# Gate phase of a hybrid decoder block: two additions made by accumulating transfers in place of VectorE

## Chip, cores and metric

One of the eight cores of a Trainium2 chip runs the program. The metric is the device time of one execution in microseconds, the median of several runs.

The core's engines run on their own and wait for each other by semaphores. In the profile PE is TensorE (PEld its weight loads), DVE is VectorE, ACT is ScalarE, POOL is GpSimd and SP is SyncE, which here only issues transfers. Each engine takes its instructions in the order in which they are written.

## Reference

The kernel computes one decoder block over 2048 tokens of width 1024. Attention and a linear recurrence run side by side; their joined output is projected, normalised and added to the input; last, a gate adds a normalised embedding. Only the end matters here:

```python
mix = jnp.concatenate([y_attn, y_lru], axis=-1) @ w_out[i]
h = h + rmsnorm(mix, post_gain[i])
e = rmsnorm(p[i] @ w_ple[i], ple_gain[i])
gate = jax.nn.sigmoid(h @ w_ple_gate[i] + b_ple_gate[i])
h = h + gate * e
```

All of it is float32, and the result is (1, 2048, 1024).

## The kernel before

The kernel works through its stages one after the other: the projections, the attention, the recurrence, the output projection, and last the gate phase, which the change is about. Every float32 operand of a matmul is split into a high and a low part, and each product is made of three matmuls (lines 66 to 68).

**The calendar.** From the output projection on, the program is written in slots. `plan(slot, phase, f)` puts a piece of work into a slot; within a slot the phases come in the order LOAD, COMBINE, PREP, JOB, MUL, GATE, STORE, and `run_slots` writes the pieces out in that order. A slot holds 12 matmuls of TensorE. This order is the order in which each engine and SP's queue take their work; the pieces themselves start when their semaphores allow.

**The gate phase** goes through 16 blocks of 128 tokens (TB = 16, n is the block). Block n's matmuls take slots s to s + 3, with s = G0 + 4n. For each block `plan_gate(n)` plans:

- `load_m` (slot s - 8; s - 10 and s - 7 for blocks 0 and 1): SP loads the projected row block from `m_d` into `mt` (2 buffers) and the input row block from `x` into `xt` (4 buffers), 512 KB each;
- `squares` (s - 6): ACT squares and sums `mt`, DVE and POOL make the factor `rs` of the norm (lines 150 and 151);
- `residual` (s - 5): DVE scales `mt` by the factor and the gain (L1777) and adds it to `xt`; `xt` is now h;
- `turn` and `turn_split` (s - 3 and s - 2): PE transposes `xt` (L1785), ACT copies the high part `h` out of the bank (L52), DVE makes the low part (L58);
- `load_e` (s - 2): SP loads the embedding's row block into `et`, one of two buffers;
- `mul` (s to s + 3): PE's 96 matmuls, two halves of 512 columns each in its bank `pbank`;
- `bias` (two slots after a half's start): DVE adds the bias to the bank, ACT takes the sigmoid (L1813);
- `finish_`: DVE multiplies gate, embedding and its norm's factor (L1817), then adds `xt`; the sum is the result, and SP stores it from `et` (L1843) in the same slot.

Additions by the helper `tt` all carry line 1629. `X`, `XT`, `MT` and `MR` are lists of buffers, and some of their names are shared: `XT[1]` is `X[11]`, so the profile shows that row as `X`. The last block is cut into halves of 512, 256 and 256 columns.

Of the kernel before, what the change touches and what calls it, by code (L numbers as in the profile page):

```python
# [11 lines left out]
AF = mybir.ActivationFunctionType  # L12
ALU = mybir.AluOpType
# [8 lines left out]
TB = S // P  # L22
# [14 lines left out]
LOAD, COMBINE, PREP, JOB, MUL, GATE, STORE = range(7)  # L37
# [12 lines left out]
def split(nc, src, hi, lo, eh, el):  # L50
    if eh == "act":
        nc.scalar.activation(hi, src, AF.Copy)  # L52
    elif eh == "dve":
        nc.vector.tensor_copy(hi, src)
    else:
        nc.gpsimd.tensor_copy(hi, src)
    eng = nc.vector if el == "dve" else nc.gpsimd
    eng.tensor_tensor(out=lo, in0=src, in1=f32(hi), op=ALU.subtract)  # L58


def mm3(nc, out, ws, xs, start, stop):


    wh, wl = ws
    xh, xl = xs
    nc.tensor.matmul(out, lhsT=wh, rhs=xh, start=start, stop=False)  # L66
    nc.tensor.matmul(out, lhsT=wh, rhs=xl, start=False, stop=False)  # L67
    nc.tensor.matmul(out, lhsT=wl, rhs=xh, start=False, stop=stop)  # L68
# [3 lines left out]
def hymba_kernel(ctx: ExitStack, tc: tile.TileContext, x, xT, pT, w_p, w_v, w_o, w_ple, w_pg,  # L72
                 w_gates, vecs, rows, mgrp, out):
    nc = tc.nc
# [10 lines left out]
    m_d = dram.tile([S, D], F32, name="m_d")  # L85
# [61 lines left out]
    def rsqrt_small(o, ss, pool, n):  # L147

        t = pool.tile([P, n], F32, name=f"rs{n}", bufs=2)
        nc.vector.tensor_scalar(t, ss, 1.0 / D, EPS, ALU.mult, ALU.add)  # L150
        nc.gpsimd.tensor_tensor(out=o, in0=t, in1=mhalf[:, :n], op=ALU.pow)  # L151
# [51 lines left out]
    def plan(slot, phase, f):  # L203


        assert (slot, phase) >= tuple(now), (slot, phase, now)
        order_[0] += 1
        heapq.heappush(calendar.setdefault(slot, []), (phase, order_[0], f))
# [415 lines left out]
    sg, vp, lw, s = [None], [None], [None, None], {}  # L624
# [731 lines left out]
    for h in range(1, NH):  # L1356
        base = t0[4 * (h - 1)]
        for p_ in range(8):
            a = base + (13, 16, 26, 28, 31, 33, 36, 38)[p_]
# [12 lines left out]
    for i, (n, k) in enumerate([(0, k) for k in range(KD)] + [(1, k) for k in range(5)]):  # L1372
        a = last0 + 2 * i
# [119 lines left out]
    X, banks = [], {}  # L1493

    def bank3():
        return ps3.tile([P, 512], F32, name="bank3")
# [62 lines left out]
    G_ = Ctx()  # L1559
# [34 lines left out]
    MR, U2_, U3_, XT, MT, A1 = [], [], [], [], [], []  # L1594
# [21 lines left out]
    def product_bank():  # L1616
        return G_.pse.tile([P, 512], F32, name="pbank")
# [11 lines left out]
    tt = lambda o, x, y, op: nc.vector.tensor_tensor(out=o, in0=x, in1=y, op=op)  # L1629
# [94 lines left out]
    for n in range(1, 12):  # L1724
        for k in range(KD):
            if n == 1 and k < 5:
                continue
            s = k - 4 if n == 1 else 11 + 3 * k // 2 if n == 2 else w_starts[n - 1] + k
# [30 lines left out]
    def plan_gate(n):  # L1759
        s = G0 + 4 * n  # L1760
        ts = slice(n * P, (n + 1) * P)
        u = Ctx()
        c_load = s - (10, 7)[n] if n < 2 else s - 8

        def load_m():
            u.mt, u.xt = MT[n % 2], XT[n % 4]
            nc.sync.dma_start(out=u.mt, in_=m_d[ts, :])
            nc.sync.dma_start(out=u.xt, in_=x[ts, :])

        def squares():  # L1770
            u.ss = G_.small.tile([P, 1], F32, name="ss", bufs=2)
            u.rs = G_.small.tile([P, 1], F32, name="rsm", bufs=2)
            nc.scalar.activation(X[8], u.mt, AF.Square, accum_out=u.ss)
            rsqrt_small(u.rs, u.ss, G_.small, 1)

        def residual():
            nc.vector.scalar_tensor_tensor(out=u.mt, in0=u.mt, scalar=u.rs, in1=G_.pgain,  # L1777
                                           op0=ALU.mult, op1=ALU.mult)
            tt(u.xt, u.mt, u.xt, ALU.add)

        def turn(q):
            b = u.b = bank3()
            for k in range(4):
                kk = 4 * q + k
                nc.tensor.transpose(b[:, k * P:(k + 1) * P], u.xt[:, kk * P:(kk + 1) * P], ident)  # L1785

        def turn_split(q):
            if q == 0:
                if n < 2:
                    G_.h[n] = [G_.r3.tile([P, 512], F32R, name=f"h{n}{i}", tag=f"mr{i}" if n else f"U{i}", bufs=1)  # L1790
                               for i in range(4)]
                h = G_.h[n % 2]
                u.h = [(h[0], h[1]), (h[2], h[3])]
            split(nc, u.b, u.h[q][0], u.h[q][1], "act", "dve")

        def mul(a, z, ks):
            if ks[0] == 0:
                u.bank = product_bank()
            for k in ks:
                c = slice(k % 4 * P, (k % 4 + 1) * P)  # L1800
                hh, hl = u.h[k // 4]
                mm3(nc, u.bank[:, :z - a], (hh[:, c], hl[:, c]), (wG[k][0][:, a:z], wG[k][1][:, a:z]),
                    k == 0, k == KD - 1)

        def load_e():
            u.et = X[9 + n % 2]
            nc.sync.dma_start(out=u.et, in_=e_d[ts, :])

        def bias(a, z, b):
            u.gt = MR[4 + turn_[0] % 4][:, :z - a]  # L1810
            turn_[0] += 1
            tt(u.gt, b[:, :z - a], G_.bgate[:, a:z], ALU.add)
            nc.scalar.activation(u.gt, u.gt, AF.Sigmoid)  # L1813
            return u.gt

        def finish_(a, z, gt):
            nc.vector.scalar_tensor_tensor(out=u.et[:, a:z], in0=gt, scalar=rstd_e[:, n:n + 1],  # L1817
                                           in1=u.et[:, a:z], op0=ALU.mult, op1=ALU.mult)
            tt(u.et[:, a:z], u.et[:, a:z], u.xt[:, a:z], ALU.add)

        plan(c_load, LOAD, load_m)
        plan(s - 6, JOB, squares)
        plan(s - 5, JOB, residual)
        for q in range(2):
            plan(s - 3 + q, GATE, lambda q=q: turn(q))
            plan(s - 3 + q, GATE, lambda q=q: turn_split(q))
        plan(s - 2, LOAD, load_e)
        cuts = ((0, 512), (512, 1024)) if n < TB - 1 else ((0, 512), (512, 768), (768, 1024))
        for j, (a, z) in enumerate(cuts):
            b_ = []  # L1830
            if z - a == 512:
                for m in range(2):
                    plan(s + 2 * j + m, MUL, lambda a=a, z=z, m=m: mul(a, z, range(4 * m, 4 * m + 4)))
                e = s + 2 * j + 2
            else:
                plan(s + 1 + j, MUL, lambda a=a, z=z: mul(a, z, range(KD)))
                e = s + 2 + j
            plan(e - 1, STORE, lambda b_=b_: b_.append(u.bank))
            g_ = []
            plan(e, COMBINE, lambda a=a, z=z, b_=b_, g_=g_: g_.append(bias(a, z, b_[0])))  # L1840
            plan(e, JOB, lambda a=a, z=z, g_=g_: finish_(a, z, g_[0]))
            plan(e, STORE if n < TB - 1 else JOB,
                 lambda a=a, z=z: nc.sync.dma_start(out=out[ts, a:z], in_=u.et[:, a:z]))  # L1843

    G_.small, G_.h = w1, {}
    for n in range(TB):
        plan_gate(n)
# [67 lines left out]
```

## Time and profile before

| | us |
|---|---|
| median of 3 runs | 2120.77 |
| lowest and highest | 2119.97, 2121.5 |
| the profiled execution | 2120.41 |
| its span, first to last instruction | 2118.6 |

TensorE's mean granted clock was 0.995 of full speed. The gate phase's transposes and matmuls stand in the span from about 1918 us to its end.

The page slices the span into 40 equal parts; each digit is the busy share of a slice in tenths:

```profile
PE   8799999999999999999999999999999999999999
DVE  7777997696758877896578888888885678776665
POOL 4834554332203334733026656566542000000000
DMA  8498898988788889887757776777744777665553
```

TensorE is nearly full throughout. POOL, which works in the first three quarters, does hardly anything in the last nine slices. In the gate phase SP's queue is the only one that kernel transfers run on.

### The profile page before, as it was taken

Reading aid. Unit: us, or ns where it says so; the run is one execution under the profiler, and the core shown is the slowest. Engines: PE = TensorE matmul, PEld = TensorE weight load, DVE = VectorE, ACT = ScalarE, POOL = GpSimd, SP = SyncE. Lnnn points to the kernel's source line nnn. Section 1 sums busy time; section 2 is a strip of 40 time slices with the busy share of each in tenths; the row PEclk is TensorE's granted clock in tenths of the full one; section 3 lists DMA queues with packets and bytes.
Section 4 is the critical chain, followed back from the end, with each engine's and each line's share of the span. In section 5 each row is a group of like instructions: output and inputs, shape, how many; then the busy total and the mean of one; then the engine's idle time right before and its main releaser. Section 6 shows DMA issues by size and latency. Waiting matters only on the chain.

```text
span 2118.6 us, 31621 instructions
## 1 busy us (share of the span) xinstructions
PE 2084.5 (98%) x10586; PEld 1744.3 (82%) x10586; DVE 1619.9 (76%) x2693; ACT 1144.9 (54%) x1871; POOL 736.2 (35%) x633
## 2 busy tenths in 40 slices
PE   8799999999999999999999999999999999999999
PEld 6788888888988888888878888888887888888887
DVE  7777997696758877896578888888885678776665
ACT  7435765443327776565267776777774344442232
POOL 4834554332203334733026656566542000000000
PEclk9999999999999999999999999999999999999999
DMA  8498898988788889887757776777744777665553
GB/s 319 180 313 294 291 347 304 343 322 308 268 276 270 279 254 299 268 280 259 267 180 225 230 210 222 235 228 230 209 159 138 247 246 240 191 217 171 182 174 119
DMA packets 274835, 518.92 MB, mean 245 GB/s; under 512 B 27104, under 2 KB 93936, under 8 KB 274672
## 3 DMA queue, kind: packets, MB, share of 16 engines
q1 hardware_dynamic: 274528, 516.86, 73.6%
q8 instruction: 83, 1.36, 0.3%
q14 instruction: 80, 0.66, 0.1%
q10 hardware_dynamic: 144, 0.05, 0.0%
HBM read 314.55 MB, written 202.25 MB: 244 GB/s over the span
## 4 chain that ended last, share of the span: by engine, by line
PE 84%; POOL 4%; DMA 4%; DVE 3%; issue 3%; ACT 1%; SPq 0%; DVEq 0%; POOLq 0%; ACTq 0%
PE bank L66 15%; PE bank L67 15%; PE bank L68 15%; PE pbank L68 7%; PE pbank L66 7%; PE pbank L67 7%; PE tbank L1263 3%; PE sbank L66 3%; PE sbank L68 2%; PE sbank L67 2%; PE obank L67 2%; PE obank L68 2%; PE obank L66 2%; POOL s L690 1%; DMA dg<-nb_d 1%
## 5 line engine op out<-in xcount | busy, mean ns | idle before, releaser
L66 PE MATMUL bank<-XH,op 128*128 128x512 f32 x876 | 347.3, 396 | 0.0
L67 PE MATMUL bank<-XL,op 128*128 128x512 f32 x876 | 346.0, 395 | 0.0
L68 PE MATMUL bank<-XH,op 128*128 128x512 f32 x876 | 345.7, 395 | 0.0
L363 DVE TENSOR_TENSOR c<-bank,c 128x512 f32<-128x512 f32 x280 | 186.8, 684 | 126.4 <-PE bank L68 120.0
L58 DVE TENSOR_TENSOR tl<-tbank,th 128x512 fp32r<-128x512 f32 (+1 forms) x320 | 192.3, 607 | 83.1 <-ACT th L52 79.3
L52 ACT ACTIVATE th<-tbank 128x512 fp32r<-128x512 f32 (+1 forms) x320 | 167.4, 529 | 119.6 <-PE tbank L1263 115.0
L68 PEld LDWEIGHTS bank<-XH,op 128*128 128x128 f32 x876 | 164.7, 188 | 39.2
L66 PEld LDWEIGHTS bank<-XH,op 128*128 128x128 f32 x876 | 164.6, 188 | 39.2 <-issue 0.5
L67 PEld LDWEIGHTS bank<-XL,op 128*128 128x128 f32 x876 | 164.7, 188 | 39.0 <-issue 0.5
L1236 ACT ACTIVATE pr<-pr,m 128x640 f32<-128x640 f32 (+7 forms) x124 | 152.0, 1226 | 45.1 <-DVE m L1227 44.4
L1263 PE MATMUL tbank<-ident,pr 128*128 128x128 f32 x1088 | 171.8, 273 | 0.0
L151 POOL TENSOR_TENSOR rsm<-rs,mhalf 128x1 f32<-128x1 f32 x16 | 8.7, 541 | 437.6 <-DVE rs L150 437.6
L1263 PEld LDWEIGHTS tbank<-ident,pr 128*128 128x128 f32 x1088 | 134.2, 140 | 28.8 <-issue 0.2
L66 PE MATMUL sbank<-kh,qh 128*128 128x512 f32 (+3 forms) x320 | 137.0, 428 | 3.7 <-DVE m L1227 2.7
L66 PE MATMUL obank<-th,vh 128*128 128x512 f32 (+1 forms) x320 | 124.0, 387 | 1.4 <-ACT th L52 1.4
L285 ACT ACTIVATE op<-wf 128x512 fp32r<-128x512 f32 (+1 forms) x96 | 60.1, 630 | 114.2 <-PE bank L68 88.6
L67 PE MATMUL obank<-tl,vh 128*128 128x512 f32 (+1 forms) x320 | 118.2, 369 | 1.4 <-DVE tl L58 0.2
L68 PE MATMUL obank<-th,vl 128*128 128x512 f32 (+1 forms) x320 | 117.5, 367 | 0.0
L68 PE MATMUL sbank<-kh,ql 128*128 128x512 f32 (+3 forms) x320 | 116.4, 364 | 0.3 <-DVE ql L1167 0.2
L67 PE MATMUL sbank<-kl,qh 128*128 128x512 f32 (+3 forms) x320 | 116.1, 363 | 0.0
L67 PE MATMUL bank<-op,XH 128*128 128x258 f32 x328 | 95.6, 292 | 8.5 <-POOL op L291 5.4
L285 ACT ACTIVATE op<-ws 128x512 fp32r<-128x512 f32 (+1 forms) x72 | 45.2, 629 | 99.3 <-PE bank L68 54.4
(319 smaller groups left out, 5838.0 us busy)
## 6 DMA issues: line engine op xcount, KB each, us to landing
wo_d<-op SPq DMA_DIRECT2D x140, 512.0 KB, 4.6
op<-wo_d SPq DMA_DIRECT2D x79, 512.0 KB, 4.9
wf<-in_w_p_dram SPq DMA_DIRECT2D x80, 256.0 KB, 4.8
wh<-wo_d SPq DMA_DIRECT2D x61, 256.0 KB, 4.2
wl<-wo_d SPq DMA_DIRECT2D x61, 256.0 KB, 4.4
vo_d<-op SPq DMA_DIRECT2D x28, 516.0 KB, 3.9
wst<-wt_d SPq DMA_DIRECT2D x56, 256.0 KB, 3.7
wst<-in_w_o_dram SPq DMA_DIRECT2D x40, 256.0 KB, 3.3
```

The lines of the kernel that those rows point to most:

```text
L52: nc.scalar.activation(hi, src, AF.Copy)
L58: eng.tensor_tensor(out=lo, in0=src, in1=f32(hi), op=ALU.subtract)
L66: nc.tensor.matmul(out, lhsT=wh, rhs=xh, start=start, stop=False)
L67: nc.tensor.matmul(out, lhsT=wh, rhs=xl, start=False, stop=False)
L68: nc.tensor.matmul(out, lhsT=wl, rhs=xh, start=False, stop=stop)
L151: nc.gpsimd.tensor_tensor(out=o, in0=t, in1=mhalf[:, :n], op=ALU.pow)
L285: nc.scalar.activation(op[:, :n], self.source(i, hf), AF.Copy)
L363: nc.vector.tensor_tensor(out=o, in0=x, in1=y, op=ALU.add)
L690: (eng or nc.gpsimd).tensor_tensor(out=o, in0=a, in1=b, op=ALU.subtract)
L1236: nc.scalar.activation(pr[0][:, :L], pr[0][:, :L], AF.Exp, bias=m2, scale=-1.0, accum_out=u.r4[:, i:i + 1])
L1263: nc.tensor.transpose(b[:, i * P:(i + 1) * P], u.P[i][:, sb * P:(sb + 1) * P], ident)
```

## The change

The input row is no longer loaded by SP. `mt` is loaded straight into the `xt` buffer, scaled there in place, and then POOL issues a transfer that adds the row of `x` from memory into it. The last sum, `et` plus `xt`, is likewise made by a transfer from `xt` to `et` with an addition, for all blocks but the last, which keeps its addition on VectorE. Squares and scaling come one slot earlier (not for block 1), the load of m one slot earlier from block 2 on, the stores of the result one slot later, and `et` rotates over three buffers, the third being the freed `MT[0]`.

```diff
-        c_load = s - (10, 7)[n] if n < 2 else s - 8
+        c_load = s - (10, 7)[n] if n < 2 else s - 9
 
         def load_m():
-            u.mt, u.xt = MT[n % 2], XT[n % 4]
-            nc.sync.dma_start(out=u.mt, in_=m_d[ts, :])
-            nc.sync.dma_start(out=u.xt, in_=x[ts, :])
+            u.xt = XT[n % 4]
+            nc.sync.dma_start(out=u.xt, in_=m_d[ts, :])
...
-            nc.scalar.activation(X[8], u.mt, AF.Square, accum_out=u.ss)
+            nc.scalar.activation(X[8], u.xt, AF.Square, accum_out=u.ss)
...
         def residual():
-            nc.vector.scalar_tensor_tensor(out=u.mt, in0=u.mt, scalar=u.rs, in1=G_.pgain,
+            nc.vector.scalar_tensor_tensor(out=u.xt, in0=u.xt, scalar=u.rs, in1=G_.pgain,
                                            op0=ALU.mult, op1=ALU.mult)
-            tt(u.xt, u.mt, u.xt, ALU.add)
+            nc.gpsimd.dma_start(out=u.xt, in_=x[ts, :], accum_op=ALU.add)
...
-            u.et = X[9 + n % 2]
+            u.et = (X[9], X[10], MT[0])[n % 3]
...
-            tt(u.et[:, a:z], u.et[:, a:z], u.xt[:, a:z], ALU.add)
+            if n == TB - 1:
+                tt(u.et[:, a:z], u.et[:, a:z], u.xt[:, a:z], ALU.add)
+            else:
+                nc.gpsimd.dma_start(out=u.et[:, a:z], in_=u.xt[:, a:z], accum_op=ALU.add)
...
-        plan(s - 6, JOB, squares)
-        plan(s - 5, JOB, residual)
+        plan(s - 7 + (n == 1), JOB, squares)
+        plan(s - 6 + (n == 1), JOB, residual)
...
-            plan(e, STORE if n < TB - 1 else JOB,
+            plan(e + 1 if n < TB - 1 else e, STORE if n < TB - 1 else JOB,
```

VectorE's order in one steady block (block 2 at its gate, block 3 at its transposes, block 4 at its scaling), before. `h` is the low part of the turned row, `mr` the gate's product with its bias, `X_18100` the buffer et, `mt_18535` and `xt_18537` block 4's row:

```order
L58 TENSOR_TENSOR h_20204<-bank_20373,h_20203 128x512
L1629 TENSOR_TENSOR mr_18119<-pbank,bgate 128x512
L1817 SCALAR_TENSOR_TENSOR X_18100<-mr_18119,rstd_e,X_18100 128x512
L1629 TENSOR_TENSOR X_18100<-X_18100,xt_18538 128x512
L150 TENSOR_SCALAR rs_20388<-ss 128x1
L58 TENSOR_TENSOR h_20206<-bank_20404,h_20205 128x512
L1777 SCALAR_TENSOR_TENSOR mt_18535<-mt_18535,rsm,pgain 128x1024
L1629 TENSOR_TENSOR xt_18537<-mt_18535,xt_18537 128x1024
L1629 TENSOR_TENSOR mr_18120<-pbank,bgate 128x512
L1817 SCALAR_TENSOR_TENSOR X_18100<-mr_18120,rstd_e,X_18100 128x512
L1629 TENSOR_TENSOR X_18100<-X_18100,xt_18538 128x512
```

The same place of the changed program, where `mt_18535` is now block 2's et:

```order
L58 TENSOR_TENSOR h_20207<-bank_20373,h_20206 128x512
L1629 TENSOR_TENSOR mr_18119<-pbank,bgate 128x512
L1816 SCALAR_TENSOR_TENSOR mt_18535<-mr_18119,rstd_e,mt_18535 128x512
L1776 SCALAR_TENSOR_TENSOR xt_18537<-xt_18537,rsm,pgain 128x1024
L58 TENSOR_TENSOR h_20209<-bank_20401,h_20208 128x512
L1629 TENSOR_TENSOR mr_18120<-pbank,bgate 128x512
L1816 SCALAR_TENSOR_TENSOR mt_18535<-mr_18120,rstd_e,mt_18535 128x512
L150 TENSOR_SCALAR rs_20442<-ss 128x1
```

The three additions are gone, the scaling has moved ahead of the second `h` row to just behind the gate's first product, and the factor's row, now of block 5, stands behind the second.

POOL's queue over the same block, where before there was one `rsm` row per block:

```order
L151 TENSOR_TENSOR rsm<-rs_20358,mhalf 128x1
L1821 DMA mt_18535<-xt_18538 128x512
L1778 DMA xt_18537<-in_x_dram 128x1024
L1821 DMA mt_18535<-xt_18538 128x512
L151 TENSOR_TENSOR rsm<-rs_20442,mhalf 128x1
```

The x addition for block 4 stands between the two last sums of block 2.

SP's queue over one block before, from block 2's second store on (then block 4's e, block 3's first store, block 6's m and x):

```order
L1843 DMA out_dram<-X_18100 128x512
L1807 DMA X_18100<-e_d 128x1024
L1843 DMA out_dram<-X_18101 128x512
L1767 DMA mt_18535<-m_d 128x1024
L1768 DMA xt_18538<-in_x_dram 128x1024
```

And after, from block 0's stores on (block 2's e, block 4's m, block 1's stores, and so on):

```order
L1845 DMA out_dram<-X_18100 128x512 x2
L1806 DMA mt_18535<-e_d 128x1024
L1767 DMA xt_18537<-m_d 128x1024
L1845 DMA out_dram<-X_18101 128x512 x2
L1806 DMA X_18100<-e_d 128x1024
L1767 DMA X_18102<-m_d 128x1024
```

The load of x has left the queue, and both stores of a block, which now wait for the sums' transfers, stand directly ahead of the load of e and the load of m.

## Prediction

> **What bounds the kernel now.** I read the page's first part, then the windows of the last stage, then the chain that ended last there. The first row gives each engine's busy time, share of the span and instructions.
>
> ```profile
> PE 2084.5 (98%) x10586; PEld 1744.3 (82%) x10586; DVE 1619.9 (76%) x2693; ACT 1144.9 (54%) x1871; POOL 736.2 (35%) x633
> ```
>
> The change touches only the gate phase, so the average says little. The window row from 1911 to 2100 us (window, its length, then busy us of PE, PE's weight loads, DVE, ACT and POOL, granted clock, DMA share, GB/s) and the chain's shares by line from 1720 us to the end say more:
>
> ```profile
> 1911.00:2100.00 189.00, 189.00 (x894) 156.07 (x893) 124.64 (x169) 52.19 (x91) 8.28 (x16) 1.00 0.52 173
> by line: PE pbank L68 31.8%; PE pbank L66 31.8%; PE pbank L67 31.7%; PE bank L1785 3.5%; DVE X L1817 0.1%; DVE mr L1629 0.1%; ACT mr L1813 0.1%; DVE X L1629 0.1%; issue 0.0%; ACTq L1813 0.0%
> ```
>
> TensorE is busy for all 189 us, at full clock, and its matmuls and transposes make up 98.8% of the chain. VectorE is busy for 66% of that time and is nowhere on the chain but in the tail of about 0.1% a piece. **Taking work from VectorE here can save nothing by itself.** The question is only whether what replaces it reaches TensorE in time.
>
> **What is removed.** These rows of the groups (names, shapes, count | busy us, mean ns | idle before) hold the additions, from 1900 us to the end:
>
> ```profile
> L1629 DVE TENSOR_TENSOR xt<-mt,xt 128x1024 f32<-128x1024 f32 x12 | 14.7, 1225 | 0.4
> L1629 DVE TENSOR_TENSOR X<-mt,X 128x1024 f32<-128x1024 f32 x4 | 4.9, 1225 | 0.1
> L1629 DVE TENSOR_TENSOR X<-X,xt 128x512 f32<-128x512 f32 (+1 forms) x25 | 16.8, 671 | 0.9
> L1629 DVE TENSOR_TENSOR X<-X,X 128x512 f32<-128x512 f32 x8 | 5.5, 692 | 0.3
> ```
>
> The first two are the input row's 16 additions, 19.6 us. The last two are the 33 last sums; three of them belong to block 15 and stay, so 30 of about 0.69 us go, 20.8 us. Together VectorE loses some 40 us, all of it beside the matmuls: gain on the path, 0.
>
> **What is added, and where it can hurt.** One steady block, DVE first, then PE's transposes (start us, length, line, tiles):
>
> ```profile
> 1980.77 0.75 DVE L1817 SCALAR_TENSOR_TENSOR X<-mr,rstd_e,X 128x512 f32<-128x512 f32 x1 [0.70 <-ACT mr L1813]
> 1981.56 0.69 DVE L1629 TENSOR_TENSOR X<-X,xt 128x512 f32<-128x512 f32 x1
> 1982.17 0.14 DVE L150 TENSOR_SCALAR rs<-ss 128x1 f32<-128x1 f32 x1
> 1982.30 0.69 DVE L58 TENSOR_TENSOR h<-bank,h 128x512 fp32r<-128x512 f32 x1
> 1983.03 1.28 DVE L1777 SCALAR_TENSOR_TENSOR mt<-mt,rsm,pgain 128x1024 f32<-128x1024 f32 x1
> 1984.35 1.23 DVE L1629 TENSOR_TENSOR xt<-mt,xt 128x1024 f32<-128x1024 f32 x1
> 1985.49 0.68 DVE L1629 TENSOR_TENSOR mr<-pbank,bgate 128x512 f32<-128x512 f32 x1
> 1986.87 0.75 DVE L1817 SCALAR_TENSOR_TENSOR X<-mr,rstd_e,X 128x512 f32<-128x512 f32 x1 [0.70 <-ACT mr L1813]
> ...
> 1977.52 0.60 PE L1785 MATMUL bank<-ident,X 128*128 128x128 f32 x4
> 1980.72 0.60 PE L1785 MATMUL bank<-ident,X 128*128 128x128 f32 x4
> 1989.37 0.60 PE L1785 MATMUL bank<-ident,xt 128*128 128x128 f32 x4
> ```
>
> A block takes 1989.37 - 1977.52 = 11.85 us. The row xt is ready at 1985.58 and transposed at 1989.37: 3.8 us of cover now. In the changed order the scaling (1.28 us) stands right behind the first scaling of the gate's product, where the last sum stood: it would run from 1981.56 to 1982.84. The factor it needs is made a slot earlier, behind the previous block's gate, so nothing new is waited for. From 1982.84 the transfer that adds x has until 1989.37: **6.53 us from issue to landing**. It is POOL's third entry in the block; ahead of it stands the transfer of the last sum, whose operand is ready at 1981.52. Behind it in POOL's queue stands only the second last sum, ready at 1987.62, so nobody else waits for it but the transposes.
>
> Blocks 0 and 1 have covers of their own:
>
> ```profile
> 1909.25 1.22 DVE L1747 TENSOR_TENSOR wa<-xt,wa 128x1024 fp32r<-128x1024 f32 x1
> 1923.28 1.28 DVE L1777 SCALAR_TENSOR_TENSOR mt<-mt,rsm,pgain 128x1024 f32<-128x1024 f32 x1
> ...
> 1918.19 0.60 PE L1785 MATMUL bank<-ident,xt 128*128 128x128 f32 x4
> 1930.06 0.60 PE L1785 MATMUL bank<-ident,X 128*128 128x128 f32 x4
> ```
>
> Block 0's scaling comes behind the L1747 row, so it would end at 1910.47 + 1.28 = 1911.75: cover 6.4 us. Block 1's keeps its place and ends at 1924.56: cover 5.5 us.
>
> No transfer of this trace adds, and none is issued by POOL, so its time has to be bounded. These are the nearest rows (KB each, median us from issue to landing; below them the smallest, median and largest landing of the tile xt, nearly all of it the x loads; then SP issuing one block's):
>
> ```profile
> X<-e_d SPq DMA_DIRECT2D x15, 512.0 KB, 3.3
> out_dram<-X SPq DMA_DIRECT2D x28, 256.0 KB, 2.0
> mt<-m_d SPq DMA_DIRECT2D x13, 512.0 KB, 4.4
> xt<-in_x_dram SPq DMA_DIRECT2D x10, 512.0 KB, 5.1
> ...
> DMA to landing us min/median/max: 4.6/5.4/7.6
> ...
> 1982.66 0.43 SPq L1767 DMA_DIRECT2D mt<-m_d  x1
> 1983.14 0.45 SPq L1768 DMA_DIRECT2D xt<-in_x_dram  x1
> 1988.38 0.34 SPq L1843 DMA_DIRECT2D out_dram<-X  x1
> ```
>
> Lower end: 3.3 us, a plain 512 KB load with nothing beside it, if the addition is free. Between 256 and 512 KB lie 1.3 us, so reading the destination as well (another 512 KB) would be 2.6 us more: 5.9 us. Upper end: the slowest x load, 7.6 us, with another 512 KB load issued 0.5 us ahead of it as at 1982.66, plus 1.3 us for the 256 KB sum ahead of it in POOL's queue: 8.9 us. POOL's own issuing time is inside these ends; SP's is 0.45 us. I take **5.9 us**, because an addition must read both operands. That is 0.6 us inside the cover of a steady block, and 0.4 us too long for block 1 alone.
>
> The Trainium skill, "Collectives: The Full Stack", section "The bandwidth ceiling: the fold count and why AG ≠ RS ≠ AR", says that an adding transfer costs twice the read traffic because it reads two sources, and measures half the rate. That speaks for the doubled read, not for the 3.3 us; no run shown here measures it.
>
> The last sum's transfers carry 256 KB each; by the same rows 2.0 + 1.3 = 3.3 us. The store of the result now stands behind them in SP's queue, and behind that store stand the load of e two blocks on and that of m four blocks on. These rows are ACT's:
>
> ```profile
> 1986.21 0.63 ACT L1813 ACTIVATE mr<-mr 128x512 f32<-128x512 f32 x1 [3.94 <-DVE mr L1629]
> 1990.00 0.60 ACT L52 ACTIVATE h<-bank 128x512 fp32r<-128x512 f32 x1 [3.16 <-PE bank L1785]
> 1980.64 1.04 ACT L1773 ACTIVATE X<-mt 128x1024 f32<-128x1024 f32 x1
> 1981.60 0.18 ACT L1773 ACTIVATION_READ_ACCUMULATOR X<-mt 128x1 f32 x1
> ```
>
> The second sum can be issued at 1987.62. The m load issues about 0.8 us (a store and a load's issue) after it lands and takes 4.4 us; its squares (1.04 us and a read of 0.18) now stand behind the sigmoid one block later and ahead of the h copy at 1990.00 + 11.85. To leave that copy alone the load must have landed by 2000.6, so the sum may take 2000.6 - 1987.6 - 0.8 - 4.4 = 7.8 us. At 3.3 it is hidden with 4.5 us to spare. The squares moved one slot forward cost nothing: ACT is busy for 52 of 189 us.
>
> In the tail only block 14's second store is new on SP's way to the end:
>
> ```profile
> 2104.15 0.75 DVE L1817 SCALAR_TENSOR_TENSOR X<-mr,rstd_e,X 128x512 f32<-128x512 f32 x1 [0.70 <-ACT mr L1813]
> 2115.44 0.42 DVE L1629 TENSOR_TENSOR X<-X,xt 128x256 f32<-128x256 f32 x1
> ```
>
> Its sum lands at 2104.90 + 3.3 = 2108.2, 7 us before the last addition starts, which itself is unchanged. So the tail costs 0.
>
> **The sum**, against the profiled execution's 2120.41 us (span 2118.6, 1.8 around it): removed 0, steady blocks 0, block 1 +0.4, tail 0: 2120.8. The runs' median, 2120.77, lies 0.4 above the profiled one, so the forecast is **2121 us, no change**. "No change" means within 0.2%, 4.2 us, about what a measurement of this kernel can tell.
>
> **Rivals.**
> 1. *The x addition lands late* (slower). Place: the first transposes of each block. Point: 6.53 us; for the 14 steady blocks together, 4.2 us are reached at 6.83. For it speaks the load on the DMA engines: a block moves 2 MiB now (m, x, e and the result) at a share of 0.52; afterwards 2.5, and with the second reads 3.5, a share of 0.52 x 3.5/2 = 0.91. SP's store and two loads start just when the sum before lands, some 3 us ahead of the x addition. Against it: they are issued early and should be mostly through. At 7.9 us: 14 x 1.4, block 1 2.4 and block 0 1.5, 23 us: 2144. At 8.9: 14 x 2.4 + 3.4 + 2.5 = 39.5: 2160. A stall also gives the loads ahead more time, so the true price is below this.
> 2. *The store behind the sum holds up SP* (slower). Point: 7.8 us for a 256 KB sum. At 10 us ACT is 2.2 us late, and so is the scaling behind it, against 0.6 us of cover: 1.6 x 14 = 22 us: 2143. Against it: three times the 3.3 us.
> 3. *POOL can't issue while VectorE runs* (slower). The two-operand scaling of 1.28 us runs while the last sum should be issued, and the 0.69 us h row follows when the x addition should. Held by both, the pair moves 1.4 us: 7.3 us, 0.8 x 14 + 1.8 + 0.9 = 14 us: 2135. Against it: VectorE is then idle until 1985.49. The Trainium skill, "SBUF — State Buffer", section "SBUF: two separate sides", has such a rule against this change: a transfer issued by GpSimd starves while VectorE holds the port pair they share in a two-port mode. By the section "Who interferes with whom" a two-tensor operation has no such mode. No row here shows either.
> 4. *Matmuls get denser with VectorE quieter* (faster). 48 matmuls and 8 transposes fill 11.85 us with no gap, so nothing points to a gain of 4.2 us.
>
> **How the numbers follow.** Hidden 0.48; late x addition 0.37; SP held up 0.07; POOL locked out 0.05; faster 0.03. The last sums not leaving VectorE isn't a case: the order shows them gone. So faster 0.03, same 0.48, slower 0.49, spread over three causes of which none is as likely as the hidden one. The range starts at 2118.5, under the fastest run shown (2119.97), and reaches 2155: that is rival 1 nearly to its bound, taken somewhat lower because a stall relieves itself, with rivals 2 and 3 inside; about 0.15 is left out.
>
> **What would show it.** Right: PE busy for the whole window from 1911 us, no idle time of PE before the L1784 transposes, x additions landing in under 6.5 us, VectorE some 40 us less busy. Wrong: PE waiting for the DMA of xt once per block (rival 1, price = landing - 6.5); ACT's squares waiting for m (rival 2); POOL's issues starting late behind VectorE's ends (rival 3). The forecast falls with the 5.9 us: it is a doubled read argued from plain loads, and 0.9 us more ends the cover.

## The result, and the profile after

| | before | after |
|---|---|---|
| median of 4 runs, us | 2120.59 | 2139.97 |
| lowest and highest, us | 2119.97, 2121.5 | 2138.69, 2142.16 |
| profiled span, us | 2118.6 | 2137.5 |

The changed kernel is slower: ratio 1.0094, 95% interval 1.0079 to 1.0109. The forecast was 2121 us and no change; what came is rival 1, the late x addition.

The page's first part (busy us, share, instructions) and its slices of the span, after:

```profile
PE 2088.0 (98%) x10586; PEld 1744.6 (82%) x10586; DVE 1579.4 (74%) x2647; ACT 1148.2 (54%) x1871; POOL 777.5 (36%) x679
...
PE   8799999999999999999999999999999999999898
DVE  7777988696758877885588878888874688763343
POOL 4834455332103335632035665656541000002221
```

VectorE has lost 1619.9 - 1579.4 = 40.5 us, just as the change intends, and POOL has gained its transfers' issuing. Yet TensorE's last slices show 8 twice where there were only nines: it waits now. The window of the gate phase, TensorE's waits before the transposes and what ended them (us in total, times, longest), and the shares of the chain from 1720 us on say where:

```profile
1911.00:2100.00 189.00, 174.84 (x804) 141.54 (x803) 77.82 (x114) 50.87 (x85) 44.40 (x56) 0.98 0.81 197
```

```profile
PE bank L1784 <- DMA xt<-in_x_dram: 8.7, 8, 1.5
PE bank L1784 <- DMA X<-in_x_dram: 6.6, 4, 3.2
```

```profile
by line: PE pbank L68 20.7%; PE pbank L67 20.6%; PE pbank L66 20.6%; DMA xt<-in_x_dram 10.3%; DMA X<-in_x_dram 7.0%; issue 6.1%; PE bank L1784 2.7%; DVE mr L1629 1.8%; ACT mr L1812 1.6%; DVE h L58 1.6%; DMA X<-X 1.3%; ACT h L52 1.2%; DMA ou
```

TensorE is busy for 174.84 of 189 us, where it was busy for all of them, and every wait before the transposes (L1784) ends with the transfer of x: 15.3 us in 12 waits. The chain shows the same transfers with 17.3%, which is far more than the waits: it counts each late transfer at its full length, most of which lies beside matmuls. What the delay costs is read from the spacing of the first transposes of the blocks. Here are those of blocks 0, 1 (with its second transposes), 2, 3, 5 and 15, the last:

```profile
1916.55 0.60 PE L1784 MATMUL bank<-ident,xt 128*128 128x128 f32 x4
...
1931.74 1.09 PE L1784 MATMUL bank<-ident,X 128*128 128x128 f32 x4 [3.16 <-DMA X<-in_x_dram]
1937.72 0.60 PE L1784 MATMUL bank<-ident,X 128*128 128x128 f32 x4
...
1946.38 0.60 PE L1784 MATMUL bank<-ident,xt 128*128 128x128 f32 x4
...
1958.24 0.60 PE L1784 MATMUL bank<-ident,xt 128*128 128x128 f32 x4
...
1984.93 0.63 PE L1784 MATMUL bank<-ident,X 128*128 128x128 f32 x4 [1.60 <-DMA X<-in_x_dram]
...
2114.93 0.63 PE L1784 MATMUL bank<-ident,xt 128*128 128x128 f32 x4
```

A block took 11.86 us before. Now:

| place | us |
|---|---|
| block 0's transposes come earlier, 1916.55 for 1918.19 (ahead of the phase; it varies between profiles) | -1.6 |
| blocks 0 to 1: 15.19 - 11.86 | +3.3 |
| blocks 1 to 2: 14.64 - 11.86 | +2.8 |
| blocks 3 to 15: 156.69 - 12 x 11.86 | +14.4 |
| sum (span: 2137.5 - 2118.6 = 18.9) | 18.9 |

Of the 14.4 us, 12.1 are the recorded waits of blocks 4 to 14; the rest, some 0.2 us a block, is not explained. The 2.8 us behind block 1 aren't a wait. The windows around that wait (length, busy PE, PEld, DVE, ACT, POOL, granted clock, DMA share, GB/s):

```profile
1928.00:1930.00 2.00, 0.57 (x3) 0.15 (x1) 0.00 (x0) 0.00 (x0) 0.00 (x0) 1.00 1.06 272
1930.00:1932.00 2.00, 0.26 (x2) 0.29 (x3) 0.00 (x0) 0.00 (x0) 0.00 (x0) 0.72 0.98 365
1932.00:1934.00 2.00, 2.00 (x8) 1.71 (x7) 0.51 (x1) 1.12 (x2) 0.00 (x0) 0.50 0.11 43
1934.00:1936.00 2.00, 2.00 (x6) 1.55 (x5) 1.30 (x3) 1.39 (x2) 0.00 (x0) 0.50 0.00 0
...
1938.00:1940.00 2.00, 2.00 (x11) 1.66 (x10) 0.69 (x1) 0.60 (x1) 0.67 (x1) 1.00 0.91 147
```

During the wait the granted clock falls, and TensorE then works at 0.50 until about 1938 us: the two turns of block 1 are 5.98 us apart in place of 3.20.

Why the transfer is late shows in one steady block, on VectorE and POOL (block 5's x addition, for which the transposes at 1984.93 wait), and in the transfers from 1926 us on:

```profile
1974.57 0.75 DVE L1816 SCALAR_TENSOR_TENSOR X<-mr,rstd_e,X 128x512 f32<-128x512 f32 x1 [0.70 <-ACT mr L1812]
1975.24 1.28 DVE L1776 SCALAR_TENSOR_TENSOR X<-X,rsm,pgain 128x1024 f32<-128x1024 f32 x1
1976.44 0.68 DVE L58 TENSOR_TENSOR h<-bank,h 128x512 fp32r<-128x512 f32 x1
...
1975.73 0.90 POOL L1821 DMA_DIRECT2D X<-xt  x1 [6.90 <-DVE X L1816]
1977.19 0.88 POOL L1778 DMA_DIRECT2D X<-in_x_dram  x1 [0.55 <-DVE h L58]
1980.47 0.86 POOL L1821 DMA_DIRECT2D X<-xt  x1 [2.40 <-DVE X L1816]
```

```profile
q0 software_dynamic: 5870, 14.35, 46.2%
q1 hardware_dynamic: 7632, 20.97, 34.0%
...
xt<-in_x_dram POOLq DMA_DIRECT2D x11, 512.0 KB, 7.0
...
X<-xt POOLq DMA_DIRECT2D x14, 256.0 KB, 4.9
```

The row is ready at 1975.24 + 1.28 = 1976.52, and the x addition is issued 0.67 us later, 1.46 us behind the last sum's. It lands in 7.0 us at the median, so 7.7 us after the row is ready: more than the 6.53 us of cover. (The row of the issue names the h row as the end of POOL's wait; the addition doesn't need that row.) All engines' orders are those that were foreseen; only this time is too long.

### The profile page after: what moved, and what is told of

Same layout as the page of the kernel before. It is cut to its first block, busy times and chain, and to the rows that moved or that the text cites. A ratio compares the mean times of both kernels' runs of the same rounds, so it can differ in the third digit from the quotient of the medians.

```text
span 2137.5 us, 31721 instructions
## 1 busy us (share of the span) xinstructions
PE 2088.0 (98%) x10586; PEld 1744.6 (82%) x10586; DVE 1579.4 (74%) x2647; ACT 1148.2 (54%) x1871; POOL 777.5 (36%) x679
## 4 chain that ended last, share of the span: by engine, by line
PE 85%; DMA 5%; DVE 4%; issue 2%; POOL 2%; ACT 2%; SPq 0%; DVEq 0%; ACTq 0%; POOLq 0%
PE bank L66 15%; PE bank L67 15%; PE bank L68 15%; PE tbank L1263 5%; PE pbank L68 5%; PE pbank L67 5%; PE pbank L66 5%; PE sbank L66 3%; PE sbank L68 3%; PE sbank L67 3%; PE obank L67 3%; PE obank L68 3%; PE obank L66 3%; DMA xt<-in_x_dram 2%; DMA X<-in_x_dram 1%
## 5 line engine op out<-in xcount | busy, mean ns | idle before, releaser
L67 PEld LDWEIGHTS bank<-XL,op 128*128 128x128 f32 x876 | 164.7, 188 | 39.1 <-issue 0.5
L151 POOL TENSOR_TENSOR rsm<-rs,mhalf 128x1 f32<-128x1 f32 x16 | 13.2, 824 | 269.9 <-DVE rs L150 269.9
```

## The experiments

The **theory** (A): the x addition stands behind a last sum's transfer on POOL's queue and so lands some 1.5 us later than alone; with the way to its issue it misses the cover in each block. **Rivals**: the doubled reads load the DMA engines so much that any transfer is late (B); SP or the sums' own length hold up the pipeline (C). Each diff is against the changed kernel; each ratio, with its 95% interval, is to the kernel before, run beside the experiment.

**1. The x addition first.** Scaling and x addition go ahead of the last sum, on VectorE and on POOL's queue.

```diff
-        plan(s - 6 + (n == 1), JOB, residual)
+        plan(s - 6 + (n == 1), PREP, residual)
```

> Only the order within a slot is changed: the scaling of the next row stands ahead of the gate's first scaling, so POOL issues the addition of x ahead of the last sum's transfer. In the changed kernel the x addition of a steady block is issued 0.67 us after its operand is ready (behind the last sum's 0.9 us issue) and lands 7.0 us later; TensorE stalls about 1.2 us in each of blocks 4 to 15 and about 6 us around block 1. Theory A (the cover is too short by what stands ahead of the x addition): the issue comes about 1.9 us earlier, the stalls of blocks 4 to 15 go (14 us), block 1's stays: 2125 to 2128 us. Theory B (the transfer engines are too full, the landing moves with them): the x addition meets more of SP's loads and takes up to 2 us longer from issue to landing, so the stalls stay and the time is 2136 to 2140 us.

Measured: 2125.33 us, ratio 1.0024 (1.0014 to 1.0033). The causes of TensorE's waits over the gate phase, one steady block, and all x additions' landings (smallest, median, largest) from 1900 us on:

```profile
PE bank L1784 <- DMA X<-in_x_dram: 3.1, 1, 3.1
```

```profile
1981.29 1.28 DVE L1776 SCALAR_TENSOR_TENSOR xt<-xt,rsm,pgain 128x1024 f32<-128x1024 f32 x1
1982.48 0.75 DVE L1816 SCALAR_TENSOR_TENSOR X<-mr,rstd_e,X 128x512 f32<-128x512 f32 x1
...
1983.23 0.89 POOL L1778 DMA_DIRECT2D xt<-in_x_dram  x1 [5.68 <-PE bank L1784]
1983.86 1.16 POOL L1821 DMA_DIRECT2D X<-xt  x1
...
1990.66 0.60 PE L1784 MATMUL bank<-ident,xt 128*128 128x128 f32 x4
```

```profile
DMA to landing us min/median/max: 5.3/5.5/8.1
```

All the steady waits are gone, and one is left, block 1's. The landing fell from 7.0 to 5.5 us, and the addition is issued 7.4 us ahead of the transposes (1990.66 - 1983.23). Both are due to the order, and this run doesn't separate them; the landing does tell A from B, since the DMA share between 1950 and 2100 us was no lower than with the sum ahead (0.90, and 0.84 in the changed kernel). B falls as their cause. The profiled execution, 2121.75 us, is the shortest of the ten; the median lies 3.6 us above it. In this profile the granted clock stays at 1.00 behind block 1's wait; whether it fell in the other executions no profile shows.

**2. Block 1's x added on VectorE**, all other blocks as in the change.

```diff
             nc.sync.dma_start(out=u.xt, in_=m_d[ts, :])
+            if n == 1:
+                nc.sync.dma_start(out=MT[1], in_=x[ts, :])
...
-            nc.gpsimd.dma_start(out=u.xt, in_=x[ts, :], accum_op=ALU.add)
+            if n == 1:
+                tt(u.xt, u.xt, MT[1], ALU.add)
+            else:
+                nc.gpsimd.dma_start(out=u.xt, in_=x[ts, :], accum_op=ALU.add)
```

> Block 1 alone gets its input row by SP and its addition on VectorE; all other blocks as in the changed kernel. Theory A (block 1's 3.2 us wait is followed by a slower granted clock, half speed for some 6 us): both go, 3.3 + 2.8 us, the steady stalls stay: 2133 to 2135 us. Rival (the slower clock near 1930 us comes from something else): only the wait goes, 2136 to 2137 us, and the transposes of block 1 are still some 6 us apart.

Measured: 2136.85 us, ratio 1.0083 (1.0068 to 1.0098), some 2 us above what the theory had and within the rival's 2136 to 2137 us. But the rival's sign, turns of block 1 some 6 us apart, is missing: they are 3.20 apart. Block 1's wait and its slow stretch are gone (first transposes at 1917.09, 1928.95 and 1940.81, 11.86 apart), but the other blocks lose more: behind block 1's transposes the excess over 11.86 a block, apart from the slow stretch there, rose from 14.4 to 19.0 us. Block 3, which didn't wait in the changed kernel, loses 1.64 us now: the delay at block 1 had bought it time, and experiment 9 shows which part of it. And two of the waits were long enough to be followed by a slow stretch. The first of these (block 5's first and second transposes), and the windows around it:

```profile
1981.44 0.63 PE L1789 MATMUL bank<-ident,X 128*128 128x128 f32 x4 [1.96 <-DMA X<-in_x_dram]
1986.26 0.60 PE L1789 MATMUL bank<-ident,X 128*128 128x128 f32 x4
```

```profile
1980.00:1982.00 2.00, 0.56 (x5) 0.59 (x6) 0.00 (x0) 0.00 (x0) 0.00 (x0) 1.00 0.46 91
1982.00:1984.00 2.00, 2.00 (x7) 1.54 (x6) 1.26 (x2) 0.60 (x1) 0.00 (x0) 0.52 0.03 5
```

A wait of 1.96 us, then 4.82 us from turn to turn in place of 3.20.

**3. The x additions alone**, all last sums on VectorE.

```diff
-            if n == TB - 1:
+            if n < TB:
```

> The last sums are back on VectorE for all blocks; only the input row is added by a transfer. VectorE reaches the scaling some 0.65 us later, POOL issues the x addition with nothing ahead of it. If the sums' transfers ahead of it in POOL's queue make it slow, it lands in 5 to 6 us from issue in place of 7.0 and the steady stalls shrink to about 0: 2125 to 2129 us. If the x addition is slow by itself or by SP's loads, it still lands in about 7 us, and the stalls stay: 2136 to 2141 us.

Measured: 2131.74 us, ratio 1.0057 (1.004 to 1.0074), between the two expectations. With no sum on the queue an x addition lands in 5.6 us at the median, so the queue's part of A is right: 1.4 us of the 7.0. But the last sum is back on VectorE ahead of the scaling, which makes the row ready some 0.7 us later, so waits of 0.2 to 1.1 us stay. Block 1 waits as before (3.13 us, landing 8.1).

**4. The last sums alone**: x is loaded by SP and added on VectorE, the sums stay transfers.

```diff
             nc.sync.dma_start(out=u.xt, in_=m_d[ts, :])
+            nc.sync.dma_start(out=MT[n > 0], in_=x[ts, :])
...
-            nc.gpsimd.dma_start(out=u.xt, in_=x[ts, :], accum_op=ALU.add)
+            tt(u.xt, u.xt, MT[n > 0], ALU.add)
```

One buffer serves all blocks from 1 on here, and block 1's row gets block 2's input.

> Only the last sums are made by transfers; the input row is loaded by SP and added on VectorE as before. If the x addition alone reaches the path, TensorE waits nowhere: 2119 to 2123 us. If the sums' transfers hold up SP's loads (rival 2 of the prediction), ACT's squares wait and PE stalls: over 2125 us.

Measured: 2120.64 us, ratio 1.0001 (0.9991 to 1.001). TensorE waits for nothing, and the sums land in 3.7 us at the median. The sums and the stores behind them cost nothing when no x addition stands beside them: C falls.

**5 and 6. Block 1 without neighbours.** In the changed kernel SP issues two loads right behind block 1's x addition, which POOL issues at 1923.47:

```profile
1924.26 0.43 SPq L1806 DMA_DIRECT2D X<-e_d  x1
1924.73 0.44 SPq L1767 DMA_DIRECT2D xt<-m_d  x1
```

This edit moves both a slot or two back, first in the changed kernel, then together with edit 1.

```diff
-        c_load = s - (10, 7)[n] if n < 2 else s - 9
+        c_load = s - (10, 7)[n] if n < 2 else s - 9 + (n == 3)
...
-        plan(s - 2, LOAD, load_e)
+        plan(s - 2 + 2 * (n == 1), LOAD, load_e)
```

> The loads of e for block 1 and of m for block 3, which SP issues within 1.3 us after block 1's x addition in the changed kernel, go behind the first store of the result. There that x addition took 8.1 us to land, block 0's, alone on the engines, 5.6. If SP's loads beside it are the cause, it lands in 5.6 to 6.5 us, TensorE waits 0.5 to 1.5 us in place of 3.2, the granted clock stays at 1.00 behind it, and the time falls by 4 to 6 us against the changed kernel, to about 2134 to 2136 us. If the long landing has another cause, it stays at 8 us and the time at 2139 to 2141 us.

> Both orders together: the x addition ahead of the last sum's transfer in every block, and SP's two loads out of block 1's way. All additions stay transfers. If the two places are all of the loss, TensorE waits only about 1 us at block 1: 2119 to 2122 us, within 0.2% of the kernel before and not below it by more than that, since VectorE's 40 us were never on the path. If something else costs time too: 2124 us or more.

Measured: 2143.59 us, ratio 1.0114 (1.0099 to 1.0129), and 2126.82 us, ratio 1.003 (1.0018 to 1.0041). The first misses both of its times, and the second falls into "something else costs time too". The landing fell from 8.1 to 6.6 us in the first, so the two loads do make it longer by 1.5 us (the 1.0 us that it still lies above block 0's 5.6 is not explained), and the wait from 3.16 to 1.63 us, with the clock at 1.00 and the turns 3.23 apart. But the load of m that was moved is block 3's, and block 3 now waits: 2.93 us in the first (turns 4.70 apart behind it), 2.47 in the second. The loss moved, and the edit says nothing on the total.

**7. The same transfer without its addition**: x is loaded over the scaled row. The normalised projection is left out of h.

```diff
-            nc.gpsimd.dma_start(out=u.xt, in_=x[ts, :], accum_op=ALU.add)
+            nc.gpsimd.dma_start(out=u.xt, in_=x[ts, :])
```

> The changed kernel's x transfer without the addition: POOL issues a plain load of x over the scaled row, so the normalised projection is left out of h. If reading the destination as well is what makes the x transfer long (a doubled read), it lands 1.3 to 2 us sooner than 7.0, at 5 to 5.7 us, and most of the steady stalls go: 2122 to 2130 us. If POOL's way of issuing or SP's loads make it long, it still lands in about 7 us: 2137 to 2141 us.

Measured: 2119.73 us, ratio 0.9996 (0.9987 to 1.0006); TensorE waits for nothing. The transfers from 1926 us on, and POOL's rows of one block:

```profile
xt<-in_x_dram POOLq DMA_DIRECT2D x11, 512.0 KB, 4.7
...
X<-xt POOLq DMA_DIRECT2D x14, 256.0 KB, 3.6
```

```profile
1982.10 0.89 POOL L1821 DMA_DIRECT2D X<-xt  x1 [5.66 <-DVE X L1816]
1983.58 0.56 POOL L1778 DMA_DIRECT2D xt<-in_x_dram  x1 [0.59 <-DVE h L58]
```

Same queue, same place, same bytes of x: 4.7 us in place of 7.0, and 0.56 us to issue in place of 0.88. The addition costs 2.3 us, and taking it out is enough to turn the loss into none. That the time goes into reading the destination, and not into the adding itself, this run doesn't show.

**8. Edits 1 and 2 together**: x first, and block 1's on VectorE.

> The changed kernel with the x addition issued ahead of the last sum (PREP instead of JOB) in every block, and block 1's x loaded by SP and added on VectorE. Theory (the two places, the x addition behind the sum in the steady blocks and block 1's landing, are the whole loss): TensorE waits for no DMA of xt in any block, x additions land in 5.5 to 5.7 us, 2119 to 2122 us. Rival (a further cost, such as transposes and matmuls slower beside a DMA share of 0.9): 2123 us or more with no wait before the transposes.

Measured: 2120.46 us, ratio 0.9996 (0.9987 to 1.0005). One wait is left in the gate phase:

```profile
PE bank L1789 <- DMA xt<-in_x_dram: 0.3, 1, 0.3
```

The two places are the whole loss, within the interval. The x additions landed in 6.2 us at the median here, which is 0.5 above what was expected and not explained; the 7.4 us from issue to transposes cover it. Here 45 of the 46 additions have left VectorE, and the time is that of before: the relief is worth nothing.

**9. Block 1's wait filled with work**: 14 matmuls ahead of its first transposes, which aren't used.

```diff
+            if n == 1 and q == 0:
+                hh = G_.h[0][0]
+                for k in range(14):
+                    nc.tensor.matmul(b, lhsT=hh[:, :P], rhs=wG[0][0][:, :512], start=True, stop=True)
```

> The changed kernel with 14 extra matmuls of high parts, 128 x 512, ahead of block 1's first transposes, into the bank that the transposes then overwrite; their result is not used. They fill TensorE's wait of 3.16 us there. Theory (the half clock behind that wait comes from TensorE being idle): turns of block 1 3.2 us apart, granted clock 1.00 behind them, 2136 to 2138 us. Rival (the clock fell for another reason, such as the transfers): clock 0.50 for some 6 us as in the changed kernel, turns about 6 us apart, 2139 to 2141 us.

Measured: 2140.22 us, ratio 1.0088 (1.0074 to 1.0102): the time missed, the clock came as the theory has it. TensorE's rows at block 1, and two windows behind them:

```profile
1930.80 3.33 PE L1785 MATMUL bank<-wg,h 128*128 128x512 f32 x14
1934.19 0.66 PE L1788 MATMUL bank<-ident,X 128*128 128x128 f32 x4
...
1937.44 0.60 PE L1788 MATMUL bank<-ident,X 128*128 128x128 f32 x4
```

```profile
1934.00:1936.00 2.00, 1.95 (x11) 1.59 (x11) 0.48 (x1) 1.10 (x2) 0.00 (x0) 1.00 0.33 129
1936.00:1938.00 2.00, 2.00 (x13) 1.67 (x12) 1.30 (x3) 1.42 (x2) 0.00 (x0) 1.00 0.00 0
```

The same delay, with TensorE busy, left the clock at 1.00 and the turns 3.25 apart: that fits a slow stretch that comes from TensorE's idleness. This run alone doesn't prove it, since the clock also stayed at 1.00 behind the unfilled 3.13 us of experiment 1. But in windows of 2 us between 1900 and 2112 us the clock fell below 0.99 at five places in all profiles of this case, each time at a wait of TensorE for an x addition: at block 1 (changed kernel and experiment 3), at block 3 where experiment 5 had moved the wait there, and at blocks 5 and 9 in experiment 2. That the transfers play no part in it isn't shown.

Of the 2.8 us saved there 1.7 came back as longer waits, as in experiment 2. Block 3 waits again (1.41 us), though block 1 is as late as in the changed kernel (15.28 us behind block 0, and 15.19 there): so it was the slow stretch, and not the lateness of the first transposes, that had bought block 3 its time. From block 0's transposes to block 15's it is 1.0 us less than in the changed kernel (197.35 and 198.38). This gate phase also began 2.4 us later, at 1918.91, which hides that gain in the time.

## Why the prediction was right and where it failed

- *Removed work is worth nothing*: right. VectorE lost 40.5 us for the 40 foreseen, and experiments 4 and 8, with 30 and with 45 of the 46 additions gone, run at the time of before.
- *The x addition takes 5.9 us*: right for an addition with nothing ahead of it. It took 5.6 us with the sums off the queue. What was put in for "an addition must read both operands", 2.6 us, was close: the addition costs 2.3 (experiment 7), though no run shows that the second read is what takes them.
- **"That is 0.6 us inside the cover of a steady block"** is the step that failed. The 6.53 us of cover were counted from the row being ready, while a landing counts from the issue: 0.67 us lie between. And the last sum ahead of it on the queue, which the upper end of the range had at 1.3 us and the value taken had not, cost 1.4. So 6.53 - 0.67 - 5.6 - 1.4 = -1.1 us, where the 11 waits behind block 3 range from 0.56 to 1.60, 1.1 at the mean. The prediction's own "0.9 us more ends the cover" held: there were 1.8 more (0.67 + 1.4 - 0.3). For the same reason its test "price = landing - 6.5" reads 0.5 us a block and is short by the way to the issue.
- *"0.4 us too long for block 1 alone"*: the place was right, the term was mis-sized; it cost 6.1 us. The addition was issued at 1923.47, 4.9 us ahead of the transposes that were due at 1928.41 (1916.55 + 11.86), where 5.5 us of cover were counted, and it landed in 8.1 us: 3.2 too long. Two loads of SP that were issued right behind it make 1.5 of the landing (experiment 5). The lower clock behind the wait, 2.8 us, was in no case of the prediction.
- *Rival 1, late x additions*: it happened, at the place described, while the case held likeliest, that the transfer stays hidden, did not. Its size came out by luck in part. By its own sum the landings measured, 7.0 us and 8.1 at block 1, cost 14 x 0.47 + 2.6, some 9 us; the phase lost 20.5 (3.3 + 2.8 + 14.4), close to the 23 that the sum gives for a landing of 7.9 us. The way to the issue and the slower clock, neither of which it had, made up for the shorter landing. "A stall also gives the loads ahead more time" held for the slow stretch behind block 1's wait, after which two blocks ran without a wait, and not for the wait by itself (experiments 2 and 9).
- *Last sums and SP's queue (rival 2)*: rightly put aside. The sums took 4.8 us for the 3.3 foreseen, within the 7.8, and experiment 4 puts their price at nothing.
- *POOL locked out by VectorE (rival 3)*: rightly put aside. The sum at 1975.73 was issued in 0.90 us while the scaling ran, the one at 1980.47 in 0.86 with VectorE idle, both 0.4 us behind their operand. What the x addition's 0.67 us consist of stays open. VectorE at work doesn't explain them: block 0's was issued at 1910.75, 0.73 us behind its scaling's end, with VectorE idle, and block 2's of experiment 1 at 1935.40, 0.29 us behind, with VectorE at work on its next row.
- *Denser matmuls (rival 4) and the tail*: nothing came of either; the last block's transposes to the span's end took 22.6 us, and 22.5 before.

What stays open: whether an x addition waits for the sum ahead of it because a queue works in order, or because both share the DMA engines for a while. For the order speaks that in experiment 1 the sum issued 0.6 us behind an x addition doesn't make it longer (5.5 us, and 5.6 with no sums in experiment 3).

## What to carry to other kernels

Work that is taken from an engine off the critical path is worth nothing by itself, and the transfer that replaces it must land inside the cover that the engine's operation had: count that cover from the issue, not from the operand, and put in whatever stands ahead on the same queue. Put the transfer that the bounding engine waits for ahead of those that nobody waits for. An edit that removes one stall may only hand its length to the next, so look at the spacing of all blocks before booking the gain.

## What the runs showed of the hardware

- **A transfer that adds takes nearly twice the DMA engines' time of one that doesn't.** 512 KB from memory took 7.0 us with the addition and 4.7 without, on the same queue at the same place. POOL's queue (q0), whose transfers of this phase all add, moved 14.35 MB in packets that took 46.2% of the DMA engines' time, SP's plain transfers (q1) 20.97 MB in 34.0%: twice the time for each byte. These queues carry different kinds of transfer, but POOL's queue alone says nearly the same. Over the same 184 us (1926 to 2110) 7.87 MB of x took 26.7% with the addition (experiment 3); without it x and the sums together took 39.1% (7), and the same sums alone 24.5% (4), which leaves 14.6% for x: 1.8 times. The Trainium skill, "Collectives: The Full Stack", section "The bandwidth ceiling: the fold count and why AG ≠ RS ≠ AR", has an adding transfer cost twice the read traffic. These rows agree in the time, here within one core; no row of them counts the reads.
- **TensorE's clock halves after waits well under 3 us, and not after all of them.** With the clock falling to 0.5 behind them: 3.16 us (changed kernel), 3.13 (experiment 3), 2.93 (5), 1.96 and 1.90 (2). With the clock staying at 1.00: 3.13 us (1), 2.47 (6), 1.95 (9), 1.88 (5), 1.85 (2) and all shorter ones. It cost 1.5 to 2.8 us each time. The Trainium skill, "TensorE: Matmul & The Clock Gate", section "What's actually happening", says that the hardware watches a free-running window of about 3.4 us; that fits that the same 3.13 us ended both ways. The advice of the Trainium skill to have "No PE-idle gaps >~3µs between matmul bursts" (same page, section "Why this matters for your kernels") is too mild by these rows: 1.90 us was enough.
- **POOL's small operation slows behind its transfers.** The norm's factor (L151) took 0.56 us at 1920.00 and 0.88 at 1981.03, right behind an issue; with no sums on the queue (experiment 3) no one of the sixteen took more than 0.56. Nobody waited for it here.
